# A two-layer encoder on one core: modulation weights loaded two items ahead at one even pace, and the second sequence's norm beside the first's last attention projection

## The chip, the cores and the metric

One core of a Trainium2 chip runs the whole program as one launch. The metric is device time in microseconds, the median of the runs. Five engines work side by side, each on its own list of instructions in order: TensorE (PE in the profile, its weight loads PEld), VectorE (DVE), ScalarE (ACT), GpSimd (POOL) and SyncE (SP). Weights come from DRAM: SP issues the loads of the projection weights, POOL those of the modulation weights and of parked rows.

## The reference

Two sequences of 512 tokens and width 1024 pass through the same two layers. A layer is a mixer and an MLP, each behind an RMS norm whose scale, shift and gate come from a condition vector `c`:

```python
def adaln(c, w, b):                       # w: 1024 x 6144, a layer
    mod = silu(c) @ w + b
    return split(mod, 6)                  # sh1, sc1, g1, sh2, sc2, g2

for i in range(2):
    sh1, sc1, g1, sh2, sc2, g2 = adaln(c, mod_w[i], mod_b[i])
    h = rmsnorm(x, norm1_g[i]) * (1 + sc1) + sh1
    m = retention(h, ...) if i == 0 else attention(h, ...)
    x = x + g1 * m
    h = rmsnorm(x, norm2_g[i]) * (1 + sc2) + sh2
    x = x + g2 * (square(relu(h @ w1)) @ w2)
return rmsnorm(x, final_g)
```

Retention has 4 heads (q and k of 256, v and a gate g of 512 columns a head), attention has 8 query heads and 2 key/value heads of 128.

## The kernel before

Everything is float32. An activation or weight tile of 128 x 512 is cut into a high and a low part (`split`, and `load_piece` for a weight piece of 128 x 1024: `whi` on ACT, `wlo` on DVE, line 206), and every product is three matmuls (`mm3`, lines 218 to 220).

**Retention** runs in eight steps, four heads of the first sequence and then four of the second. A step makes scores (`scores`, whose four evictions on DVE are line 517), values (4 weight pieces), the gate (4 pieces, evicted by line 533), the head's output `y` (line 549 and on), then the next head's q and k (4 pieces, with rope) in turn with four transposed products `tz` (PE line 570, DVE line 572), and the output projection `out` (4 pieces, evicted by line 586). That is 16 weight pieces a step. Step 3 also makes the second sequence's first norm (lines 261 to 291) and step 7 the first sequence's second norm (lines 310 to 313). In the text, a step runs from its first score eviction on DVE to that of the next step.

**Modulation** hides behind these steps. It is 12 chunks (6 a layer) of 8 items; an item is 128 columns, whose weights are two tiles of 128 x 512 (two loads, line 407, on POOL's queue) and which DVE multiplies and sums with the condition rows in two dots a sequence (`dot`, line 382): two dots where one sequence is left to do, otherwise four. Items wait in the list `bg`. Each weight piece calls `tick` behind its `wlo`; `tick` adds `pace` to a counter, and when that passes 1 it issues the dots of the item that is loaded (`bg_dot`) and then the loads of the next one (`bg_load`). The tiles come from the pool `f2` of eight, of which six are held (two rope tables, four condition tiles) until the last rope, in step 6. So one pair is left, and an item's loads wait on POOL for the dots of the item before. The scheduler keeps this program order where it must, and sets the place of each instruction on its engine by its own estimates.

**The wide MLP** (from about 1000 to 1600 us and from about 2060 us on) and **attention** follow. In attention the heads of the first sequence (`heads`: softmax and its product, 16 turns) are woven with a generator `fill`, one step of it a turn: the rest of the first sequence's last projection `p1` (rope and transposes), the second sequence's norm `nm1` (statistics, spread, then eight modulated tiles: lines 288, 290 and 291), its projection `q2` and then `q0`.

Of the kernel before, what the change touches and what calls it, by code (L numbers as in the profile page):

```python
# [18 lines left out]
EPS = 1e-6  # L19
ORDER_FIRST = "q0 q1 z0 q2 z1 z2 q3 z3"  # L20
ORDER = "g1 g2 g3 q0 z0 q1 z1 q2 z2 z3 q3"
PACE = 0.55
PACE_LAST = 1.0
SQ_W = 8
SQ_RAW = 3
SQ_SUM = 4
# [5 lines left out]
def kernel(  # L32
# [98 lines left out]
    def small(w):  # L131
        return sm.tile([P, w], F32, tag=f"s{w}", name=f"s{w}")
# [13 lines left out]
    bg, loaded = [], []  # L146
    pace = [0.0, 0.0]

    def bg_dot():
        if loaded:  # L150
            f, hv = loaded.pop()
            f(hv)

    def bg_load():
        if bg:
            f, g = bg.pop(0)
            loaded.append((g, f()))

    def tick(ins):
        pace[1] += pace[0]  # L160
# [4 lines left out]
            pace[1] -= 1.0  # L165

    def flush():
        while bg or loaded:
            bg_dot()
            bg_load()  # L170

    sq = {}

# [71 lines left out]
    def fetch(src, alloc=xtile, eng=nc.gpsimd):  # L245
        t = alloc()
        eng.dma_start(t, src)
        return t
# [53 lines left out]
    def stats_of(tiles):  # L302
        st = Stats()
        for x in tiles:
            st.add(x)
        return st
# [55 lines left out]
    def cond_row(s):  # L362
        halves = []
        for hf in range(2):
            c, th = sftile(), sftile()
            ld(c[0:1, :], cs[s:s + 1, hf * T:(hf + 1) * T])
            act(th[0:1, :], c[0:1, :], AF.Tanh, scale=0.5)
            stt(c[0:1, :], th[0:1, :], 1.0, c[0:1, :], ALU.add, ALU.mult)
            ps = abank()
            mm(ps, ones[0:1, :], c[0:1, :], start=True, stop=True)  # L370
            w = f2tile()
            act(w, ps, AF.Copy)
            halves.append(w)
        return halves
# [4 lines left out]
    def dot(a, w, cb, k):  # L379
        for hf in range(2):  # L380
            junk = sm.tile([P, T], BF16, tag="junk", name="junk", bufs=1)
            stt(junk, w[hf], 0.5, cb[hf], ALU.mult, ALU.mult, accum_out=a[:, 2 * k + hf:2 * k + hf + 1])  # L382

    def mod_cols(a, layer, ch, s, k0, k1):
        col = modc[layer, ch, s]
        av = a.rearrange("p (k t) -> p k t", t=2)
        c0 = layer * 48 + ch * KD
        c = col[:, k0:k1]
        tt(c, av[:, k0:k1, 0], mb_sb[:, c0 + k0:c0 + k1], ALU.add)
        tt(c, c, av[:, k0:k1, 1], ALU.add)  # L390
        gi = gain_of.get((layer, ch))
        if gi is not None:
            stt(c, c, 1.0, gn_sb[:, gi, k0:k1], ALU.add, ALU.mult)

    def new_col(layer, ch, s):
        modc[layer, ch, s] = const.tile([P, KD], F32, name=f"mc{layer}_{ch}_{s}")

    def mod_chunk(cb, layer, ch, seqs=(0, 1), alt=False):
        accs = {s: small(2 * KD) for s in seqs}
        for s in seqs:  # L400
            new_col(layer, ch, s)

        def load(k):
            get = xtile if alt and k % 2 else f2tile
            hv = [get(), get()]
            for hf in range(2):
                nc.gpsimd.dma_start(hv[hf], modw[layer, ch * KD + k][:, hf * T:(hf + 1) * T])  # L407
            return hv

        def step(k, hv):  # L410
            for s in seqs:
                dot(accs[s], hv, cb[s], k)
            if k == KD - 1:
                for s in seqs:
                    mod_cols(accs[s], layer, ch, s, 0, KD)

        for k in range(KD):
            bg.append((lambda k=k: load(k), lambda hv, k=k: step(k, hv)))

# [22 lines left out]
    def decay_strip(h, alloc=None):  # L444
        get = ld if alloc else nc.gpsimd.dma_start
        alloc = alloc or ftile
        d = dp.tile([P, 896], F32, tag="d", name="dstrip")
        for hf in range(2):
            sl = slice(hf * 448, (hf + 1) * 448)
            a, b = alloc(), alloc()  # L450
            get(a[:, 0:448], posneg[0][:, sl])
            get(b[:, 0:448], posneg[1][:, sl])
            nc.gpsimd.tensor_scalar(a[:, 0:448], a[:, 0:448], lg[:, h:h + 1], 0.0, ALU.mult, ALU.add)
            nc.gpsimd.tensor_scalar(b[:, 0:448], b[:, 0:448], lg[:, 4 + h:5 + h], 0.0, ALU.mult, ALU.add)
            strip_pool[0] = nc.gpsimd.tensor_tensor(d[:, sl], a[:, 0:448], b[:, 0:448], ALU.add)
            act(d[:, sl], d[:, sl], AF.Exp)
        return d
# [641 lines left out]
    def run(g, n=None):  # L1099
        while n is None or n > 0:  # L1100
            try:
                next(g)
            except StopIteration:
                return
            if n is not None:
                n -= 1
# [15 lines left out]
    cb = [cond_row(0), None]  # L1122
# [32 lines left out]
    for i in range(4):  # L1155
        for t in range(2):
            k = 2 * i + t
# [59 lines left out]
    for step in range(8):  # L1217
        s, n = divmod(step, 4)
        nm = None
        r.scores(n, strip)  # L1220
        if step == 3:
            with tc.issue_after(first_pool.ins):
                s1 = stats_of(fetch(xs[1][k]) for k in range(KD))
            nm = Norm(s1, lambda k: fetch(xs[1][k]),
                      modc[0, 1, 1], modc[0, 0, 1], True)
            r1 = Ret(1, None, nm.h)
        if step == 7:
            nm = Norm(stats_of(fetch(park[0][k]) for k in range(KD)), lambda k: fetch(park[0][k]),
                      modc[0, 4, 0], modc[0, 3, 0], True, keep=hparks[0][0])
            m.h[0] = nm.h  # L1230
        if step > 0:
            r.v(n)
        if nm is not None:
            nm.a()
        r.g(n, [0] if step else [3])
        if nm is not None:
            nm.c()
        r.y(n)
        if nm is not None:
            nm.m()  # L1240
        if step < 7:
            strip = decay_strip((n + 1) % 4)
        if step == 7:
            r.g(n, [1, 2, 3])
        if step < 7:
            nxt = r1 if step == 3 else r
            n1 = (n + 1) % 4
            for t in (ORDER if step else ORDER_FIRST).split():
                i = int(t[1])
                if t[0] == "q":  # L1250
                    nxt.qk(n1, i)
                elif t[0] == "z":
                    r.tz([i])
                else:
                    r.g(n, [i])
            if step == 0:
                flush()
                mod_chunk(cb, 0, 1, (1,))
                mod_chunk(cb, 0, 0, (1,))
                pace[0] = PACE  # L1260
            if step == 2:
                flush()
                mod_chunk(cb, 0, 2, (1,))
                for ch in (4, 3, 5):
                    mod_chunk(cb, 0, ch)
                for ch in (1, 0, 2, 3, 4, 5):
                    mod_chunk(cb, 1, ch)
                pace[0] = PACE_LAST
            if step == 3:
                while len(bg) > 71 or (loaded and len(bg) == 72):  # L1270
                    bg_dot()
                    bg_load()
            if step == 6:
                while len(bg) > 47 or (loaded and len(bg) == 48):
                    bg_dot()
                    bg_load()
            if step == 3:
                r.out(n, lambda o: nc.gpsimd.dma_start(park[0][o], x0[o]))
                r1.x = [fetch(xs[1][k], ptile) for k in range(KD)]
                r = r1  # L1280
            else:
                r.out(n)
        else:
            m.x[1] = r.x
            m.ups(0, 0, [0])
            r.tz([0, 1])
            m.ups(0, 0, [1])
            r.tz([2, 3])
            m.ups(0, 0, [2])
            st1 = Stats()  # L1290
            r.out(n, lambda o: st1.add(r.x[o]))
            with tc.issue_after(r.last.ins):
                m.x[0] = [fetch(park[0][k], ftile, nc.scalar) for k in range(KD)]
            m.ups(0, 0, [3])
            flush()
    f2_ctx.__exit__(None, None, None)
    wide_stage(m, st1)
# [28 lines left out]
    nm1 = Norm(st[1], lambda k: fetch(park[1][k]), modc[1, 1, 1], modc[1, 0, 1], True)  # L1326
    a1 = Att(1, nm1.h, tabs)
    p2, p0, p1 = a0.proj(2), a0.proj(0), a0.proj(1)
    q2, q0, q1 = a1.proj(2), a1.proj(0), a1.proj(1)

    def part(g, n):
        for _ in range(n):
            run(g, 1)
            yield
# [13 lines left out]
    run(zipped(p0, p1))  # L1348

    def fill():  # L1350
        yield from p1
        yield from nm1.steps(4)
        yield from part(q2, 4)
        yield from zipped(q2, q0)

    f = fill()
    weave(a0.heads(), f)
    run(f)
# [20 lines left out]
    f = fill()  # L1379
# [21 lines left out]
    f = finish(0, st[0])  # L1401
# [159 lines left out]
```

## Time and profile before

| what | us |
|---|---|
| median of 3 runs (2665.93 to 2669.35) | 2667.32 |
| the profiled execution | 2666.18 |
| its span, first to last instruction | 2664.4 |
| PE busy | 2528.7 (95%) |
| DVE busy | 1991.8 (75%) |
| ACT busy | 1120.2 (42%) |
| POOL busy | 526.2 (20%) |

Shares of the whole span hide the stages: a stage in which PE waits for DVE shows only in windows of that stage. Busy time of PE is also longer while the granted clock is low, so both are read together. In the views, `f` and `xf` are tiles (the pools' names without numbers), `pm`, `pa`, `ps` and `pt` are banks of PSUM, `junk` is the unused product of a dot, and a wait is named by the line that waits and the line or load that ended it. Each dot is two entries of line 382, the product and a short read of its sum.

### The profile page before, as it was taken

The page shows a single profiled execution, that of the slowest core. Times are in us where ns is not written, and L with a number is a line of the kernel's source. Part 1 is how long each engine was busy: PE and PEld are TensorE (multiplying, and loading weights), DVE is VectorE, ACT ScalarE, POOL GpSimd, SP SyncE. Part 2 cuts the span into 40 slices and gives each one's busy share as a digit, 9 for nine tenths or more (in the row PEclk, how much of TensorE's full clock was granted, in tenths as well). Part 3 has the DMA queues.
Part 4 walks back from the last instruction along what each step waited for, and adds up shares of the span by engine and source line. Part 5 has one row for each costly group of instructions (what it writes and reads, how often), then busy time and mean ns, then how long its engine had stood idle before and what let it go on. Part 6 is the DMA issues. An engine that isn't in the chain of part 4 may idle for free. (4 is left out here: it accounts for less than half of the span.)

```text
span 2664.4 us, 32643 instructions
## 1 busy us (share of the span) xinstructions
PE 2528.7 (95%) x11186; PEld 2056.7 (77%) x11186; DVE 1991.8 (75%) x3800; ACT 1120.2 (42%) x1949; POOL 526.2 (20%) x947
## 2 busy tenths in 40 slices
PE   6999999889897999999999999899999999999998
PEld 4888887767676777888878887678778788878887
DVE  6767577778877978666778867776876766688777
ACT  3433333222222355444444434675774444454432
POOL 2302112221212212121222200000014121242100
PEclk9999999999998999999999999899999999999999
DMA  7544454644444656444565434122337454474433
GB/s 248 190 127 138 126 168 148 205 143 146 134 150 132 210 181 213 163 154 163 171 211 164 162 114 140 53 63 76 115 122 271 157 180 144 160 277 159 139 95 103
DMA packets 133994, 414.00 MB, mean 155 GB/s; under 512 B 21250, under 2 KB 24194, under 8 KB 133828
## 3 DMA queue, kind: packets, MB, share of 16 engines
q0 software_dynamic: 68352, 224.58, 24.9%
q1 hardware_dynamic: 59284, 180.32, 21.6%
q10 hardware_dynamic: 6192, 7.02, 0.8%
q8 instruction: 88, 1.44, 0.2%
q14 instruction: 78, 0.64, 0.1%
HBM read 332.15 MB, written 79.69 MB: 155 GB/s over the span
## 5 line engine op out<-in xcount | busy, mean ns | idle before, releaser
L218 PE MATMUL pm<-r,whi 128*128 128x512 f32 x768 | 306.7, 402 | 29.8 <-DVE f L572 14.6
L205 ACT ACTIVATE whi<-raw 128x1024 fp32r<-128x1024 f32 x174 | 183.6, 1057 | 339.1 <-DMA raw<-in_wri_dram 106.4
L220 PE MATMUL pm<-r,wlo 128*128 128x512 f32 x768 | 304.6, 397 | 9.1 <-DVE wlo L206 9.1
L219 PE MATMUL pm<-r,whi 128*128 128x512 f32 x768 | 305.6, 398 | 5.5 <-DVE r L313 5.4
L382 DVE SCALAR_TENSOR_TENSOR junk<-f,f 128x512 bf16<-128x512 f32 x344 | 239.6, 696 | 94.1 <-DMA f<-in_modw_dram 91.0
L206 DVE TENSOR_TENSOR wlo<-raw,whi 128x1024 fp32r<-128x1024 f32 x174 | 216.9, 1247 | 89.6 <-ACT whi L205 89.0
L225 ACT ACTIVATE wh<-rawq 128x512 fp32r<-128x512 f32 x228 | 142.5, 629 | 286.6 <-PE pm L667 159.7
L225 ACT ACTIVATE wh<-sum 128x512 fp32r<-128x512 f32 x208 | 129.9, 629 | 280.0 <-PE pa L667 178.2
L666 PE MATMUL pa<-r,wh 128*128 128x512 f32 x624 | 242.7, 389 | 0.0
L667 PE MATMUL pa<-r,wh 128*128 128x512 f32 x624 | 242.7, 389 | 0.0
L668 PE MATMUL pa<-r,wh 128*128 128x512 f32 x624 | 242.7, 389 | 0.0
L407 POOL DMA_DIRECT2D f<-in_modw_dram x200 | 108.2, 541 | 596.6 <-DVE junk L382 495.8
L218 PEld LDWEIGHTS pm<-r,whi 128*128 128x128 f32 x768 | 147.3, 192 | 65.0 <-issue 15.9
L666 PE MATMUL pm<-r,wh 128*128 128x512 f32 x468 | 182.6, 390 | 1.9 <-ACT wh L225 1.9
L668 PE MATMUL pm<-r,wh 128*128 128x512 f32 x468 | 182.1, 389 | 0.0
L667 PE MATMUL pm<-r,wh 128*128 128x512 f32 x468 | 182.1, 389 | 0.0
L220 PEld LDWEIGHTS pm<-r,wlo 128*128 128x128 f32 x768 | 147.7, 192 | 42.2 <-DVE wlo L206 11.2
L218 PE MATMUL pa<-whi,r 128*128 128x512 f32 x440 | 174.2, 399 | 5.1 <-ACT whi L205 4.2
L219 PEld LDWEIGHTS pm<-r,whi 128*128 128x128 f32 x768 | 147.9, 193 | 39.8 <-DVE r L313 8.7
L219 PE MATMUL pa<-wlo,r 128*128 128x512 f32 x440 | 174.0, 396 | 0.6 <-DVE wlo L206 0.6
L226 DVE TENSOR_TENSOR wh<-sum,wh 128x512 fp32r<-128x512 f32 x208 | 141.4, 685 | 44.1 <-ACT wh L225 42.7
L220 PE MATMUL pa<-whi,r 128*128 128x512 f32 x440 | 173.6, 394 | 0.0
(277 smaller groups left out, 5978.8 us busy)
## 6 DMA issues: line engine op xcount, KB each, us to landing
rawq<-in_w_dram SPq DMA_DIRECT2D x144, 512.0 KB, 3.9
f<-in_modw_dram POOLq DMA_DIRECT2D x200, 256.0 KB, 3.4
raw<-in_wri_dram SPq DMA_DIRECT2D x92, 512.0 KB, 3.8
r<-hhpark POOLq DMA_DIRECT2D x142, 256.0 KB, 4.1
hhpark<-f POOLq DMA_DIRECT2D x96, 256.0 KB, 2.9
hhpark<-p POOLq DMA_DIRECT2D x88, 256.0 KB, 2.3
raw<-in_wro_dram SPq DMA_DIRECT2D x32, 512.0 KB, 3.7
xf<-park POOLq DMA_DIRECT2D x48, 256.0 KB, 3.4
```

Of the source, the lines that this page charges most:

```text
L205: act(hi, raw, AF.Copy)
L206: ins = tt(lo, raw, hi.bitcast(F32), ALU.subtract)
L218: mm(ps, a[0], b[0], start=first, stop=False)
L219: mm(ps, a[0], b[1], start=False, stop=False)
L220: return mm(ps, a[1], b[0], start=False, stop=last)
L225: split.last = act(hi, src_f32, AF.Copy)
L226: split.dve = tt(lo, src_f32, hi.bitcast(F32), ALU.subtract)
L382: stt(junk, w[hf], 0.5, cb[hf], ALU.mult, ALU.mult, accum_out=a[:, 2 * k + hf:2 * k + hf + 1])
L407: nc.gpsimd.dma_start(hv[hf], modw[layer, ch * KD + k][:, hf * T:(hf + 1) * T])
L666: mm(ps, a[0], b[0], start=first and k == 0, stop=False, **more)
L667: mm(ps, a[0], b[1], start=False, stop=False, **more)
L668: mm(ps, a[1], b[0], start=False, stop=k == n - 1, **more)
```

## The change

In the modulation, `PACE` 0.55 (steps 0 to 2) and `PACE_LAST` 1.0 (from the end of step 2) become one pace of 0.88 over all 96 items that are left after step 0. `bg_load` may keep two items loaded where their tiles come from different pools: items carry a `home`, and the first four chunks of layer 1 take every second item's tiles from the pool `x` of three buffers, which the norms of steps 3 and 7 use too. The chunks of layer 0, and the last two of layer 1, still have the one pair of `f2`. The flushes become `bg_until(n)`, which empties the list to n items. In attention, `fill` takes one step of `p1` and one of `nm1` a turn, four turns in all, where it took seven.

```diff
-PACE = 0.55
-PACE_LAST = 1.0
+PACE = 0.88
...
     def bg_dot():
         if loaded:
-            f, hv = loaded.pop()
+            f, hv, _ = loaded.pop(0)
             f(hv)
 
     def bg_load():
-        if bg:
-            f, g = bg.pop(0)
-            loaded.append((g, f()))
+        while bg and (not loaded or (len(loaded) == 1 and loaded[0][2] != bg[0][2])):
+            f, g, home = bg.pop(0)
+            loaded.append((g, f(), home))
+
+    def bg_until(n):
+        while len(bg) + len(loaded) > n:
+            bg_dot()
+            bg_load()
...
     def flush():
-        while bg or loaded:
-            bg_dot()
-            bg_load()
+        bg_until(0)
...
-            bg.append((lambda k=k: load(k), lambda hv, k=k: step(k, hv)))
+            bg.append((lambda k=k: load(k), lambda hv, k=k: step(k, hv), alt and k % 2))
...
                 mod_chunk(cb, 0, 0, (1,))
-                pace[0] = PACE
-            if step == 2:
-                flush()
                 mod_chunk(cb, 0, 2, (1,))
                 for ch in (4, 3, 5):
                     mod_chunk(cb, 0, ch)
                 for ch in (1, 0, 2, 3, 4, 5):
-                    mod_chunk(cb, 1, ch)
-                pace[0] = PACE_LAST
+                    mod_chunk(cb, 1, ch, alt=ch < 4)
+                pace[0] = PACE
+            if step == 2:
+                bg_until(80)
             if step == 3:
-                while len(bg) > 71 or (loaded and len(bg) == 72):
-                    bg_dot()
-                    bg_load()
+                bg_until(72)
             if step == 6:
-                while len(bg) > 47 or (loaded and len(bg) == 48):
-                    bg_dot()
-                    bg_load()
+                bg_until(48)
...
     def fill():
-        yield from p1
-        yield from nm1.steps(4)
+        h1 = nm1.steps(4)
+        for i in range(4):
+            run(p1, 1)
+            run(h1, 1)
+            yield
+        run(p1)
+        run(h1)
         yield from part(q2, 4)
         yield from zipped(q2, q0)
```

Each engine's number of instructions is the same in both. DVE's order holds these dots in steps 1 to 6 and behind the first score of step 7: before 18, 22, 44, 64, 64, 66 and 54; now 28, 39, 52, 62, 56, 56 and 33. Lines 206 to 1068 of the kernel before stand two lines lower in the changed one.

The first place is POOL's list of loads in step 5. Before, each pair of `f2` follows the other, all in the same two buffers:

```order
L407 DMA f2_5428<-in_modw_dram 128x512
L407 DMA f2_5429<-in_modw_dram 128x512
L407 DMA f2_5470<-in_modw_dram 128x512
L407 DMA f2_5471<-in_modw_dram 128x512
L407 DMA f2_5512<-in_modw_dram 128x512
L407 DMA f2_5513<-in_modw_dram 128x512
```

Now a pair of `f2` and a pair of `x` take turns, and because `x` has a third buffer, one tile of each `x` pair is loaded a turn earlier still:

```order
L409 DMA f2_5606<-in_modw_dram 128x512
L409 DMA f2_5607<-in_modw_dram 128x512
L409 DMA xf_5649<-in_modw_dram 128x512
L409 DMA xf_5861<-in_modw_dram 128x512
L409 DMA f2_5706<-in_modw_dram 128x512
L409 DMA f2_5707<-in_modw_dram 128x512
L409 DMA xf_5862<-in_modw_dram 128x512
L409 DMA xf_5987<-in_modw_dram 128x512
```

What moved: the load of an item now stands behind the dots of the item two before it, not of the one before.

The second place is DVE in step 5, from the end of the head's statistics to the first gate evictions (L554 to L557 is the chain that scales the head's output). Before:

```order
L241 SCALAR_TENSOR_TENSOR s4_5719<-s4_5718 128x4
L382 SCALAR_TENSOR_TENSOR junk_5807,s16_3097<-f2_5769,f2_162 128x512
L242 SCALAR_TENSOR_TENSOR s4_5717<-s4_5719,s4_5717 128x4
L382 SCALAR_TENSOR_TENSOR junk_5809,s16_3097<-f2_5770,f2_171 128x512
L557 SCALAR_TENSOR_TENSOR s4_5728<-s8_5650,s4_5717 128x4
L382 SCALAR_TENSOR_TENSOR junk_5811,s16_3098<-f2_5769,f2_923 128x512
L382 SCALAR_TENSOR_TENSOR junk_5813,s16_3098<-f2_5770,f2_928 128x512
L382 SCALAR_TENSOR_TENSOR junk_5853,s16_3097<-f2_5815,f2_162 128x512
L206 TENSOR_TENSOR wlo_5950<-raw_5947,whi_5949 128x1024
L533 SCALAR_TENSOR_TENSOR f_5798<-f_5798,pm_5773 128x512
```

Now:

```order
L243 SCALAR_TENSOR_TENSOR s4_5807<-s4_5806 128x4
L244 SCALAR_TENSOR_TENSOR s4_5805<-s4_5807,s4_5805 128x4
L559 SCALAR_TENSOR_TENSOR s4_5816<-s8_5738,s4_5805 128x4
L208 TENSOR_TENSOR wlo_6030<-raw_6027,whi_6029 128x1024
L535 SCALAR_TENSOR_TENSOR f_5890<-f_5890,pm_5865 128x512
L384 SCALAR_TENSOR_TENSOR junk_6033,s16_1422<-f2_5941,f2_162 128x512
```

What moved: no dot stands in this chain any more; the weight piece and the gate's eviction stand ahead of the next four dots.

The third place is PE among the first heads of attention, where the second sequence's first projection (`pa`, L218 before, L220 now) begins. `pt` and `ps` are the heads' own work. Before it is PE's row 7024:

```order
L1064 MATMUL pt_15129<-ident_92,p_14950 128x128
L218 MATMUL ps_15071<-r_14256,r_14800 128x512
L219 MATMUL ps_15071<-r_14257,r_14800 128x512
L220 MATMUL ps_15071<-r_14256,r_14801 128x512
L218 MATMUL pa_15182<-whi_15188,r_15017 128x512
L1064 MATMUL pt_15138<-ident_92,p_14911 128x128
```

Now it is row 6936:

```order
L220 MATMUL ps_14793<-r_14247,r_14475 128x512
L221 MATMUL ps_14793<-r_14248,r_14475 128x512
L222 MATMUL ps_14793<-r_14247,r_14476 128x512
L1066 MATMUL pt_14869<-ident_92,p_14647 128x128
L1066 MATMUL pt_14869<-ident_92,p_14660 128x128
L220 MATMUL pa_15024<-whi_15030,r_14841 128x512
L1066 MATMUL pt_14878<-ident_92,p_14621 128x128
```

What moved: the projection begins 88 PE instructions earlier. On DVE the low part of the first modulated tile, for which the three-matmul product waits, comes 76 instructions behind the heads' first maximum, where it came 121 behind it. From the end of this stage on, and in the wide MLP, the lists are the same.

## Rows read from the trace of the kernel before

**Rows 1.** Page: span, PE, granted clock in 40 slices.

```profile
span 2664.4 us, 32643 instructions
PE 2528.7 (95%) x11186; PEld 2056.7 (77%) x11186; DVE 1991.8 (75%) x3800; ACT 1120.2 (42%) x1949; POOL 526.2 (20%) x947
...
PEclk9999999999998999999999999899999999999999
```

**Rows 2.** Busy time by engine in steps 1 to 7 (header names the columns).

```profile
core 0: us, PE busy (x) PEld busy (x) DVE busy (x) ACT busy (x) POOL busy (x), PEclk, DMA share, GB/s
...
168.00:273.10 105.10, 105.10 (x473) 87.16 (x472) 67.78 (x122) 32.16 (x42) 16.70 (x28) 1.00 0.44 134
273.10:383.10 110.00, 108.23 (x485) 89.32 (x485) 68.99 (x129) 32.29 (x42) 18.86 (x32) 1.00 0.44 136
383.10:506.80 123.70, 110.91 (x481) 88.65 (x480) 99.40 (x210) 42.53 (x59) 37.45 (x63) 0.97 0.55 179
506.80:628.60 121.80, 112.06 (x472) 89.95 (x471) 98.11 (x223) 31.69 (x42) 26.77 (x46) 0.95 0.50 158
628.60:751.60 123.00, 109.79 (x472) 88.73 (x472) 97.48 (x221) 31.65 (x43) 25.26 (x43) 0.96 0.46 145
751.60:877.50 125.90, 109.82 (x462) 88.14 (x463) 96.16 (x221) 31.28 (x42) 26.24 (x45) 0.95 0.45 144
877.50:975.00 97.50, 89.21 (x384) 70.69 (x383) 89.44 (x219) 44.55 (x66) 24.20 (x45) 0.96 0.62 198
```

**Rows 3.** Waits of DVE in steps 4 to 6: total, times, longest.

```profile
DVE junk L382 <- DMA f<-in_modw_dram: 70.4, 46, 4.5
```

**Rows 4.** Waits of PE in steps 4 to 6.

```profile
PE pm L218 <- DVE f L572: 14.6, 3, 5.0
PE pm L218 <- DVE f L533: 7.1, 2, 4.8
PE pm L220 <- DVE wlo L206: 5.4, 3, 2.3
```

**Rows 5.** Timeline of DVE and of POOL, 638 to 652 us.

```profile
641.57 0.69 DVE L382 SCALAR_TENSOR_TENSOR junk<-f,f 128x512 bf16<-128x512 f32 x1
...
645.91 0.69 DVE L382 SCALAR_TENSOR_TENSOR junk<-f,f 128x512 bf16<-128x512 f32 x1 [3.64 <-DMA f<-in_modw_dram]
...
641.83 0.54 POOL L407 DMA_DIRECT2D f<-in_modw_dram  x1 [5.50 <-DVE junk L382]
642.56 0.54 POOL L407 DMA_DIRECT2D f<-in_modw_dram  x1 [0.20 <-issue]
```

**Rows 6.** Windows, steps 4 to 6: the six stretches at low clock.

```profile
584.40:591.20 6.80, 4.62 (x11) 3.69 (x12) 6.66 (x15) 1.58 (x2) 1.14 (x3) 0.50 0.50 155
...
sum 37.60, PE 25.77 PEld 20.23 DVE 29.80 ACT 10.72 POOL 10.49; mean PE 4.30 PEld 3.37 DVE 4.97 ACT 1.79 POOL 1.75
```

**Rows 7.** Windows of line 382 alone, step 4; two entries a dot.

```profile
506.80:628.60 121.80, 46.01 (x130) 0.95 0.50 158
```

**Rows 8.** Waits of DVE for these loads, step 3, then steps 1 and 2.

```profile
DVE junk L382 <- DMA f<-in_modw_dram: 10.8, 7, 4.7
...
DVE junk L382 <- DMA f<-in_modw_dram: 7.0, 4, 2.4
```

**Rows 9.** Waits of PE in step 7.

```profile
PE pm L219 <- DVE r L313: 5.4, 7, 1.1
PE pm L279 <- DVE f L273: 2.2, 1, 2.2
```

**Rows 10.** Windows of the first sequence's heads; one row of PE's timeline.

```profile
1696.60:1727.00 30.40, 23.14 (x89) 15.53 (x89) 26.09 (x80) 23.43 (x70) 0.54 (x1) 0.78 0.04 9
1727.00:1748.30 21.30, 16.47 (x81) 11.68 (x81) 18.75 (x43) 16.22 (x33) 3.23 (x6) 1.00 0.32 99
1748.30:1800.00 51.70, 51.65 (x256) 41.98 (x255) 38.47 (x95) 41.45 (x92) 0.54 (x1) 1.00 0.15 46
...
1747.98 0.50 PE L218 MATMUL pa<-whi,r 128*128 128x512 f32 x1 [0.98 <-ACT r L290]
```

## The prediction

> **What bounds the kernel now.** I read the page first. PE is busy for 2528.7 of 2664.4 us, and its clock is a 9 in almost every slice [rows 1], so all that a change of order can win is PE's 136 us of idle time and what the low clock costs. Then the windows by step show where that lies. In step 1 PE is busy for the whole 105.10 us, at a granted clock of 1.00. Steps 4 to 6 do the same work and take 121.8, 123.0 and 125.9 us, and here the vector engine (DVE) is busy for 98.11, 97.48 and 96.16 us [rows 2]. The waits of DVE in these three steps name one thing: 70.4 us, in 46 waits, for the modulation weights [rows 3]. Its busy time, 291.8 us, and these waits make 362.2 of 370.7 us. So DVE has no slack there, and PE waits for what DVE delivers late: the transposed products (line 572), the gate (line 533), the low weight parts (line 206) [rows 4].
>
> The timeline shows how a wait comes about. A dot, the last of its item, starts at 641.57 us; POOL, which had waited for the dots, issues the next two loads at 641.83 and 642.56; the next item's first dot starts at 645.91, after 3.64 us in which DVE did nothing [rows 5]. With one pair of tiles that stall lies between any two items that come close together. A wait of PE costs a second time: in the last 2 us of the gap of 5.0 us before line 218 [rows 4] the granted clock falls to 0.50, which is 1.2 GHz, and stays there for 6.8 us; PE works for 4.62 us of them [rows 6], at half its rate, so 2.3 us more are lost.
>
> **The change part by part.** The sum starts from the profiled execution, 2666.2 us (span 2664.4, 1.8 around it); the median of the runs shown is 1.1 above.
>
> *Steps 4 to 6, what could be won.* PE is busy for 112.06, 109.79 and 109.82 us, so it idles for 9.7, 13.2 and 16.1: 39.0. In the six stretches at the low clock PE works for 25.77 us [rows 6]; half of that, 12.9, is the clock's. Without both the three take 318.8 us, 106.3 each, which fits the 105.1 and 108.2 us of PE work in steps 1 and 2. So 51.9 us are the most that these steps can give.
>
> *Steps 4 to 6, DVE's new list.* A dot costs 46.01 us over 65 of them, 0.71 [rows 7]. There are now 62, 56 and 56 where there were 64, 64 and 66, so 1.4, 5.7 and 7.1 us go, and the list is 96.7, 91.8 and 89.1 us long. The stall was 70.4 us over 48.5 items of four dots, 1.45 an item. In the order, the first five items of step 4 and the last seven of step 6 still have one pair. If each pays 1.45 again (bounds: nothing, and the 4.5 of the longest wait), the list with its stalls is 104.0, 91.8 and 99.3 us. For items with two pairs I take no stall (bounds: none, and 1.45 again): a load comes 4.3 us behind the dot that frees its tiles [rows 5], and between that dot and the one that needs it stands a whole item, four dots of 0.71, besides the weight piece, and an even pace leaves 14 items to a step. All three lists are now shorter than PE's 106.3, so PE becomes the bound.
>
> *What stays idle.* Not everything goes, since DVE's work comes in bunches. The nearest rows are step 2, where DVE is busy for 68.99 us and PE idles for 1.8, and step 7, where DVE is busy for 89.44 of 97.5 us and PE idles for 8.3 [rows 2]; 7.6 us of step 7's waits come from its norm [rows 9], which steps 4 to 6 don't have. By the length of their lists I leave 7, 4 and 6 us, the clock's share in them: 17 (bounds: 0, as in step 1, and 30, three times some 10 for a step like step 7 with its clock). So steps 4 to 6 give 51.9 - 17 = **35 us**.
>
> Weighed against a page: by the Trainium skill, "Perfetto Trace Analysis", section "Identifying the Most-Contended Engine", busy time of matmuls is no fair measure of how near TensorE is to its limit, and that of weight loads is. By weight loads, step 1 is full at 87.16 of 105.10 us, 0.829, and steps 4 to 6 hold 266.8 us of them [rows 2], so their floor is 321.7 and not 318.8, and the most to be won 49.0; the sum would end at 2633. Here the two agree within 3 us, because the clock's share has been taken out of the busy time first; read plainly, 331.7 us busy of 370.7, it would have left only 39.0 to win.
>
> *Steps 1 to 3, which get the dots that steps 4 to 7 lose.* Step 1 gains 10 dots, 7.1 us, against 37.3 us in which DVE is idle: nothing. Step 2 gains 17 dots, 12.1 us, and seven of its items now have four dots on one pair, at most 7 x 1.45 = 10.2 us of stalls; DVE goes from 68.99 to about 91 of 110 us [rows 2]. That is like step 5, where I leave 4 us, and 1.8 are there already: cost 2 (bounds: 0 and 10, a loss like step 7's). Step 3 gains 8 dots, 5.7 us, and its 13 items on one pair pay about 18.9 us of stalls where 10.8 are seen [rows 8]: 13.8 us more on an engine that is busy for 99.40 us and waits 10.8 for loads out of 123.7, so 13.5 us of other waiting can cover it. Those waits stand elsewhere in the step than the dots, so I take a third: cost **4** (bounds: 0 and 13.8).
>
> *Step 7.* 33 dots instead of 54: 14.9 us less on DVE. PE idles there for 8.3 us, and the clock of 0.96 adds 2 to 4 [rows 2], but 5.4 of it stands at the norm's low parts and 2.2 at its spread [rows 9], and two items are still dotted between those lines. I take **4** (bounds: 0 and 11). The flushes cost nothing: at 0.88 the items that each calls for are done before it.
>
> *Attention.* The heads of the first sequence start at 1696.6. Up to 1727 PE idles for 7.3 of 30.4 us at a clock of 0.78, up to 1748.3 for 4.8 of 21.3, and then hardly at all [rows 10], because the second sequence's projection starts at 1747.98 and fills every gap. That start waits for the norm's first low part, 121 DVE instructions behind the heads' first maximum, and now 76. At the same pace, 51.4 x 76/121 = 32 us, it comes at about 1729. Of the 4.8 us, the part behind 1729 goes: **4**. The first 30 us stay as they are, since DVE is busy there for 26.09 of 30.4 us and its list only becomes denser. Bounds: 5 us won, and 7 lost, if the projection's matmuls stand in PE's list ahead of the heads' work and wait for DVE as long as PE waits now up to 1727.
>
> *The sum.* 2666.2 - 35 + 2 + 4 - 4 - 4 = 2629; with the 1.1 us between profile and median, **2630**.
>
> **The rivals.**
> - *Nothing stays idle.* Steps 4 to 6 run at 106.3 us each, as steps 1 and 2 do. For it: the order of PE's work is that of steps 1 and 2, where DVE keeps up. Against it: there DVE's list is 65% of the step, here 85 to 99%. 17 us more than forecast, and the 4 of step 3: about 2609.
> - *DVE stays the pace.* The wait for loads goes, but the transposed products and the gate still come late, because rope, evictions and dots fall into the same part of a step. For it: PE's largest waits are for these [rows 4]. Against it: DVE reached them late after some 20 us of stalls a step. With 40 us left instead of 17, 2653.
> - *Slower: the stall moves.* All items between 16 and 47 have one pair and most now have four dots. If each waits as long as the longest did, 4.5 us, step 3's list is 105.1 + 13 x 4.5 = 163.6 us against 123.7 (40 lost), step 2's 81.1 + 31.5 = 112.6 (3 lost), step 4's 96.7 + 22.5 = 119.2 (3 won) and step 6's 120.6 (5 won); step 5 wins 14 and the rest 8: 2680. It decides from a mean wait of about 4.1 us. Against it: the mean is 1.45, and the pace is lower than the one under which that was seen.
> - *No change.* PE's waits in steps 4 to 6 have another cause, and only attention and step 7 give a little: 2662 to 2667. Against it: 362 of 371 us of DVE are accounted for.
>
> **How the numbers follow.** Forecast 0.64, nothing idle 0.15, DVE the pace 0.12, no change 0.04, slower 0.05. The likeliest's own range is 2614 to 2646. The range 2604 to 2655 takes in most of the first three. A measurement of this kernel tells about 0.2% (5 us) from no change; that gives faster 0.90, same 0.05, slower 0.05.
>
> **What would show it.** Right: in steps 5 and 6 DVE's waits for modulation weights fall below 10 us a step from 23, PE is idle for less than 8 us each, and each takes 107 to 114 us; step 3 stays between 122 and 132; step 7 loses a few us; the second sequence's projection starts some 20 us earlier after the heads begin. Wrong: steps 4 to 6 keep 120 us with DVE busy for all of it, or waits for those weights of 20 us and more appear in steps 2 and 3, and PE's gaps with them.

## The result and the profile after

| | us |
|---|---|
| before, median of 4 runs (2662.38 to 2669.35) | 2666.62 |
| changed, median of 4 runs (2615.62 to 2628.67) | 2625.09 |
| ratio, with its 95% interval | 0.984 (0.9811 to 0.9869) |
| the changed kernel's profiled execution, and its span | 2615.62, 2613.8 |

The profiled execution is the fastest of the four, 9.5 us under their median. A second profile of the same kernel, taken with the experiments, has a span of 2620.7; where one execution could mislead, both are given.

The page after (its head, PE's line and the granted clock) answers to [rows 1]:

```profile
span 2613.8 us, 32647 instructions
PE 2518.2 (96%) x11186; PEld 2052.8 (79%) x11186; DVE 1992.3 (76%) x3800; ACT 1119.3 (43%) x1949; POOL 522.2 (20%) x947
PEclk9999999999999999999999999999999999999999
```

DVE does the same work, 1992 us; PE's idle time fell from 135.7 to 95.6 us, and its busy time by 10.5. About half of these 10.5 us is the clock's, if half of the time at the low clock is lost, as the prediction takes it: at 0.50 PE was busy for 70.9 us of the whole span before and is for 60.6 now, and half of the difference is 5.2. What makes up the rest isn't shown. The windows of steps 0 to 7 after (columns as in [rows 2]; the last one ends at the same PE instruction as the last row there):

```profile
99.00:170.40 71.40, 69.51 (x313) 56.79 (x312) 57.98 (x123) 20.95 (x28) 21.75 (x36) 1.00 0.57 179
170.40:277.80 107.40, 105.94 (x476) 87.51 (x475) 74.77 (x144) 32.27 (x42) 22.02 (x38) 1.00 0.50 155
277.80:386.00 108.20, 107.92 (x482) 88.67 (x481) 81.24 (x163) 31.99 (x42) 19.82 (x34) 1.00 0.47 147
386.00:518.10 132.10, 115.67 (x473) 89.43 (x473) 102.91 (x230) 41.06 (x58) 37.88 (x66) 0.92 0.54 174
518.10:630.30 112.20, 106.81 (x473) 86.86 (x473) 95.72 (x219) 33.01 (x43) 26.39 (x43) 1.00 0.54 167
630.30:733.10 102.80, 102.80 (x463) 85.19 (x462) 93.34 (x203) 31.93 (x42) 21.99 (x38) 1.00 0.54 162
733.10:841.20 108.10, 107.54 (x482) 88.72 (x481) 90.64 (x199) 32.03 (x42) 23.04 (x40) 1.00 0.52 160
841.20:931.10 89.90, 85.20 (x375) 69.36 (x375) 76.30 (x176) 43.45 (x65) 18.78 (x35) 0.98 0.58 179
```

Steps 4 to 6 take 323.1 us where they took 370.7. In step 5 PE is busy for all of its 102.8 us while DVE is still busy for 93.34 of them: the bound has changed hands. Step 3 went the other way, from 123.7 to 132.1. The waits of DVE and of PE in steps 4 to 6 after show the same, beside [rows 3] and [rows 4]:

```profile
DVE junk L384 <- DMA f<-in_modw_dram: 16.6, 12, 3.7
```

```profile
PE pa L221 <- DVE r L228: 2.3, 1, 2.3
PE pa L220 <- DVE r L228: 1.5, 1, 1.5
PE pm L572 <- DVE f L473: 1.1, 2, 0.5
```

70.4 us of waits for modulation weights have become 16.6 (10.7 in step 4, 6.0 in step 6, none in step 5; 18.6 in the second profile), and the long waits of PE for transposed products and the gate are gone. POOL's and DVE's timelines after, in step 5, show how:

```profile
639.10 0.54 POOL L409 DMA_DIRECT2D f<-in_modw_dram  x1 [6.63 <-DVE junk L384]
639.84 0.54 POOL L409 DMA_DIRECT2D f<-in_modw_dram  x1 [0.20 <-issue]
```

```profile
639.58 0.69 DVE L384 SCALAR_TENSOR_TENSOR junk<-xf,f 128x512 bf16<-128x512 f32 x1
643.53 0.69 DVE L384 SCALAR_TENSOR_TENSOR junk<-f,f 128x512 bf16<-128x512 f32 x1
```

DVE goes on at 639.58 with the other pair (`xf`), and its four dots and a weight piece fill the time until 643.53, when the first dot on the new pair of `f` runs without a wait. It is tight: 3.7 us after the second load was issued.

In step 3, PE's largest wait before and after, and the two stretches at the low clock after (windows, columns as before):

```profile
PE pm L279 <- DVE f L273: 4.7, 1, 4.7
```

```profile
PE pm L281 <- DVE f L275: 6.0, 1, 6.0
```

```profile
418.10:428.30 10.20, 5.91 (x12) 4.01 (x13) 7.06 (x21) 0.60 (x1) 1.07 (x2) 0.50 0.60 179
489.80:500.00 10.20, 7.84 (x17) 5.24 (x18) 7.92 (x16) 0.84 (x2) 3.22 (x6) 0.50 0.60 200
```

Line 281 (279 before) is the spread of the second sequence's norm. 16 dots of step 3 stand ahead of it in both kernels, and 27 now stand ahead of the norm's first low part, where 20 stood. Of the 8.4 us that step 3 lost, 3.6 are idle time of PE (12.8 before, 16.4 now) and 4.8 are busy time: the granted clock fell from 0.97 to 0.92, and the kernel before had one stretch of 6.8 us at the low clock in this step and the first 0.9 us of another.

The heads of attention, from the first maximum at 1655.1 on, and PE's row at which the projection begins, beside [rows 10]:

```profile
1655.10:1685.50 30.40, 23.83 (x96) 15.74 (x96) 27.64 (x84) 25.34 (x73) 1.08 (x2) 0.83 0.06 18
1685.50:1706.80 21.30, 21.30 (x108) 17.36 (x107) 20.34 (x44) 17.86 (x35) 3.22 (x6) 1.00 0.26 75
```

```profile
1682.79 0.50 PE L220 MATMUL pa<-whi,r 128*128 128x512 f32 x1 [1.29 <-ACT r L292]
```

The projection starts 27.7 us behind the heads' beginning, 51.4 before; the 4.8 us of idle time in the second stretch are gone, the first stretch is as it was.

### The profile page after: what moved, and what is told of

Its sections match the earlier page's. It is cut to its first block, busy times and chain, and to the rows that moved or that the text cites. A ratio compares the mean times of both kernels' runs of the same rounds, so it can differ in the third digit from the quotient of the medians.

```text
span 2613.8 us, 32647 instructions
## 1 busy us (share of the span) xinstructions
PE 2518.2 (96%) x11186; PEld 2052.8 (79%) x11186; DVE 1992.3 (76%) x3800; ACT 1119.3 (43%) x1949; POOL 522.2 (20%) x947
## 5 line engine op out<-in xcount | busy, mean ns | idle before, releaser
L220 PE MATMUL pm<-r,whi 128*128 128x512 f32 x768 | 304.2, 399 | 13.3 <-ACT r L1180 5.8
L208 DVE TENSOR_TENSOR wlo<-raw,whi 128x1024 fp32r<-128x1024 f32 x174 | 214.6, 1234 | 94.3 <-ACT whi L207 93.7
L384 DVE SCALAR_TENSOR_TENSOR junk<-f,f 128x512 bf16<-128x512 f32 x280 | 194.3, 694 | 52.1 <-DMA f<-in_modw_dram 49.2
L409 POOL DMA_DIRECT2D f<-in_modw_dram x168 | 90.7, 540 | 474.5 <-DVE junk L384 378.2
L220 PEld LDWEIGHTS pm<-r,whi 128*128 128x128 f32 x768 | 145.9, 190 | 48.3 <-ACT r L1180 6.2
L220 PE MATMUL pa<-whi,r 128*128 128x512 f32 x440 | 174.4, 399 | 5.5 <-ACT whi L207 4.2
```

The source lines that it names most:

```text
L208: ins = tt(lo, raw, hi.bitcast(F32), ALU.subtract)
L220: mm(ps, a[0], b[0], start=first, stop=False)
```

## The experiments

**Theory A**, the prediction's: the load stall made DVE late, the second pair takes it away, and then PE is the pace in steps 4 to 6. **Rival B**: the lower, even pace does it alone. The further letters stand in the expectations. The times of the kernels are medians, the columns of steps come from one profile each; 2663.2, 2663.3 and 2665.0 are those of the kernel before beside the three groups of runs (the first four kernels below, the next three, the last four). The table is what the text below reads: widths of steps from the first score evictions, the dots between those of step 3, and "step 7", from there to the first product of the wide MLP's own stage (line 666 before).

| kernel | us | ratio (95%) | dots, step 3 | step 3 | steps 4-6 | step 7 |
|---|---|---|---|---|---|---|
| before | | | 44 | 123.7 | 370.7 | 193.4 |
| changed, again | 2624.3 | 0.9853 (0.9836-0.9870) | 52 | 132.4 | 327.4 | 186.9 |
| one pair | 2650.3 | 0.9949 (0.9935-0.9964) | 52 | 133.3 | 353.5 | 187.4 |
| old paces | 2633.5 | 0.9880 (0.9861-0.9899) | 67 | 140.2 | 339.9 | 181.0 |
| old fill | 2628.3 | 0.9870 (0.9852-0.9888) | 52 | 132.5 | 327.3 | 189.5 |
| rest in step 3 | 2600.1 | 0.9764 (0.9739-0.9789) | 39 | 119.6 | 322.2 | 186.8 |
| tiny dots | 2575.4 | 0.9668 (0.9643-0.9692) | 51 | 116.6 | 313.6 | 183.9 |
| no load wait | 2679.6 | 1.0066 (1.0047-1.0085) | 49 | 119.2 | 313.4 | 186.8 |
| even step 3 | 2605.5 | 0.9780 (0.9764-0.9796) | 44 | 126.3 | 320.8 | 185.6 |
| rest only | 2614.3 | 0.9812 (0.9795-0.9829) | 40 | 122.6 | 325.5 | 191.4 |
| rest in 3 and 7 | 2597.1 | 0.9752 (0.9736-0.9768) | 39 | 118.5 | 321.8 | 186.6 |
| all two pairs | 2606.8 | 0.9788 (0.9772-0.9805) | 39 | 122.2 | 316.6 | 191.8 |

### The changed kernel again

> The changed kernel once more, as the base for the runs beside it. Both theories: 2615 to 2630 us, 36 to 51 us under the kernel before; steps 4 to 6 again about 323 us together (370.7 before). If its runs spread by 10 us again, the profile should show which stage they spread in.

2624.3, with steps 4 to 6 at 327.4. Of the 7 us between its profile and the first one, 5.6 are there before step 7, most of them in step 6, where PE is idle for 3.9 us here and for 0.6 there:

```profile
734.60:846.80 112.20, 108.33 (x477) 89.12 (x476) 93.29 (x199) 31.82 (x42) 23.12 (x40) 0.98 0.50 154
```

### One pair

```diff
-                    mod_chunk(cb, 1, ch, alt=ch < 4)
+                    mod_chunk(cb, 1, ch)
```

> The even pace of 0.88 is kept, all modulation items have the one pair of tiles again. Theory A (the loads' stall was what made the vector engine late, and the second pair takes it away): 62, 56 and 56 dots plus 1.45 us of stall for each of 14 to 15 items a step make a list of about 117, 112 and 110 us, so steps 4 to 6 take about 342 us in place of 323, the waits for modulation weights there come back to some 60 us, and the kernel takes 2640 to 2648 us. Rival B (the even pace alone did it, by taking dots out of steps 4 to 6): within 5 us of the changed kernel, 2620 to 2630.

The waits come back as A said, 58.1 us in steps 4 to 6 (waits of DVE), and with them PE's waits for the transposed products, 15.1 us after 14.6 in the kernel before [rows 4]:

```profile
DVE junk L384 <- DMA f<-in_modw_dram: 58.1, 45, 3.8
```

```profile
PE pm L220 <- DVE f L574: 15.1, 3, 5.4
```

The windows of these steps are those of a late DVE, with a lower clock:

```profile
519.00:640.20 121.20, 110.67 (x473) 90.05 (x472) 94.15 (x215) 32.91 (x43) 25.25 (x43) 0.94 0.50 155
640.20:757.20 117.00, 109.26 (x477) 88.72 (x476) 92.41 (x203) 31.94 (x42) 24.02 (x38) 0.97 0.46 143
757.20:872.50 115.30, 107.87 (x470) 88.01 (x469) 92.69 (x203) 31.93 (x42) 25.12 (x40) 0.97 0.48 152
```

B falls. The even pace has a share all the same: with one pair steps 4 to 6 take 353.5 us, 17.2 less than before, and step 3 pays 9.6 for it. A's 342 us were 11 too few, though the waits have the size that it gave: in step 5 DVE's busy time, 92.4, and its 19.5 us of waits for loads make 111.9 of the 117.0, and its other waits come on top.

### Old paces

```diff
-PACE = 0.88
+PACE = 0.55
+PACE_LAST = 1.0
...
-                bg_until(80)
+                bg_until(72)
+                pace[0] = PACE_LAST
```

> The second pair of tiles is kept, the two old paces are back (0.55 in steps 1 and 2, 1.0 from the end of step 2). Theory A: steps 1 to 3 as in the kernel before (105, 110, 124), step 4 half with stalls, steps 5 and 6 without, together some 336 us, so with attention's part 2622 to 2632, nearly all of the gain. Rival B: dots still 64, 64 and 66 in steps 4 to 6, so they keep more than 355 us together, and the kernel takes 2648 to 2660.

Steps 4 to 6 follow A, and B falls here too: they hold 203 dots, more than the 194 of the kernel before, and take 30.8 us less than there. Step 3 doesn't follow: it holds 67 dots, not the 44 of the kernel before, and takes 140.2 us (its window):

```profile
382.30:522.50 140.20, 115.46 (x474) 88.80 (x472) 111.44 (x260) 41.32 (x58) 40.85 (x72) 0.93 0.53 172
```

The reason lies in the diff: the kernel before empties its list at the end of step 2 with 80 items still to come, and this one empties it to 72. So steps 2 and 3 get 31 and 67 dots where 22 and 44 stood, and behind the first score of step 7 only 13 are left of 54. The run brings the old paces back but not the old spread, and so it doesn't price the even spread beside two pairs.

### Old fill

```diff
-        h1 = nm1.steps(4)
-        for i in range(4):
-            run(p1, 1)
-            run(h1, 1)
-            yield
-        run(p1)
-        run(h1)
+        yield from p1
+        yield from nm1.steps(4)
```

> The changed kernel with the old order in attention (the first projection's rest first, then the second norm). Theory A: attention's part of the change is worth 4 (forecast) to 8 us (the profiles of before and after differ there by 8), so 2629 to 2633 with a changed kernel at 2625. Rival: the gaps that the earlier projection fills come back later in the stage and the old order costs nothing, within 2 us of the changed kernel.

4.0 us, as forecast, though the intervals of the two ratios overlap. The trace carries it: from the heads' first maximum to the next wide product 402.0 us here and 397.6 in the changed kernel's profile of the same group. The second stretch of the heads has its 4.8 us of idle time back:

```profile
1691.40:1712.70 21.30, 16.48 (x82) 11.75 (x81) 18.78 (x44) 16.24 (x33) 3.22 (x6) 1.00 0.33 99
```

### Rest in step 3

```diff
-PACE = 0.88
+PACE = 1.0
...
     for step in range(8):
         s, n = divmod(step, 4)
+        if step == 3:
+            pace[0] = 0.0
...
         r.g(n, [0] if step else [3])
+        if step == 3:
+            pace[0] = 1.0
...
                 bg_until(72)
+                pace[0] = 0.88
```

> The changed kernel with another spread of the same items: pace 1.0 in steps 1 and 2, none through the first five weight pieces of step 3 (where the second sequence's norm is made), 1.0 for the rest of step 3, then 0.88. On the vector engine's list step 2 gets 48 dots instead of 39, step 3 gets 39 instead of 52, 12 of them ahead of the norm's spread instead of 16. Theory A (in step 3 the vector engine is the pace, so a dot there costs its 0.71 us, and in step 2 it is not): step 3 falls from 132 to about 123, step 2 rises by 0 to 3, and the kernel takes 2614 to 2620 against 2624. Rival C (step 3's loss is the one wait for the norm's spread and the stalls of the one pair, whatever the number of dots): step 3 stays at 128 or more, and the kernel takes 2621 to 2627.

Better than A said: 24 us under the changed kernel. Step 3 lost 12.8 us; the 13 dots fewer are 6.7 us of it (line 384 is busy there for 29.39 us, 36.07 in the changed kernel's profile) and DVE's waits for loads 4.6 (6.8 after 11.4). C falls. Its window, and PE's wait for the spread:

```profile
382.10:501.70 119.60, 111.50 (x486) 90.33 (x485) 98.60 (x199) 42.64 (x59) 33.35 (x59) 0.98 0.57 184
```

```profile
PE pm L281 <- DVE f L275: 2.7, 1, 2.7
```

The other gains, 4.9 us ahead of step 3 and 5.2 in steps 4 to 6, are about what two executions of one list differ by (below). Whether the fuller steps 1 and 2 have a share in the whole is asked in "rest only".

### Tiny dots

```diff
-            stt(junk, w[hf], 0.5, cb[hf], ...
+            stt(junk[:, 0:1], w[hf][:, 0:1], 0.5, cb[hf][:, 0:1], ...
```

> Work left out: every dot multiplies one column of 512; all loads and their waits stay. Theory A (in steps 5 and 6 of the changed kernel the tensor engine is the pace, in steps 3 and 4 the vector engine): steps 5 and 6 together stay at 208 to 214 us, step 3 falls to 112 to 120 and step 4 to about 107, so some 20 us in all, 2600 to 2608. Rival D (the vector engine is still the pace everywhere, just a shorter list): each of steps 4 to 6 falls by a further 5 us or more, below 102, and the kernel goes under 2595.

It went to 2575, under both numbers, but not by D's way: DVE is busy for 64 us in steps 5 and 6 instead of some 93, and yet they take 105.2 us each, 210.4 together (210.9 and 214.6 in the changed kernel's profiles), with PE busy throughout (windows of the two steps). That is PE's pace. About half of what A had missed lies ahead of step 3, which starts 13 to 14 us earlier than in the changed kernel (372.6 against 386.0 and 387.0); 6.9 of them are there before the first score eviction of step 0 (92.1 against 99.0), so the dots at the very start have a price too.

```profile
592.40:697.60 105.20, 105.20 (x473) 87.20 (x472) 64.34 (x203) 32.26 (x42) 21.94 (x38) 1.00 0.51 159
697.60:802.80 105.20, 105.20 (x473) 87.21 (x472) 64.38 (x205) 32.26 (x42) 23.02 (x40) 1.00 0.52 164
```

### No load wait

```diff
-            stt(junk, w[hf], 0.5, cb[hf], ...
+            stt(junk, cb[hf], 0.5, cb[hf], ...
```

> Data changed: every dot reads a condition tile in place of the loaded weights, so no dot waits for a load; the loads are still issued, and the number and length of the dots stay. Theory A (in steps 3 and 4, whose items still have one pair, the 12 us of waits for loads in each are on the path): step 3 falls from 132 to 120 to 125 and step 4 from 113 to about 108, the kernel takes 2606 to 2614. Rival E (these waits only take the place of others, since the tensor engine is waited for there too): less than 5 us, 2619 to 2626.

Neither: 55 us slower than the changed kernel. Steps 3 and 4 did fall, to 119.2 and 104.0, as A said. But steps 0 to 2 rose to 80.1, 132.9 and 153.9 us. POOL's timeline shows loads with nothing to hold them but the landing of the one before, and behind them in its list the tables of the next head's decay strip (line 453; the scores are multiplied by the strip). ACT waits for the strip, and behind ACT's wait stand the gate's tanh and with it DVE's eviction and PE (rows of POOL, ACT and PE):

```profile
256.39 0.54 POOL L409 DMA_DIRECT2D f<-in_modw_dram  x1 [1.06 <-DMA f<-in_modw_dram]
257.95 0.54 POOL L409 DMA_DIRECT2D f<-in_modw_dram  x1 [1.03 <-DMA f<-in_modw_dram]
258.48 0.54 POOL L453 DMA_DIRECT2D f<-in_posneg_dram  x1
```

```profile
265.39 0.58 ACT L458 ACTIVATE dstrip<-dstrip 128x448 f32<-128x448 f32 x1 [36.75 <-POOL dstrip L457]
```

```profile
269.56 0.80 PE L220 MATMUL pm<-r,whi 128*128 128x512 f32 x1 [25.92 <-DVE f L535]
```

The lists aren't those of the changed kernel: since no dot needs a load here, 93 loads stand ahead of the second strip's tables in POOL's list, where the changed kernel has 38, and 169 ahead of the third's, where it has 66. So the loss is that of another order, and the run doesn't price the stalls for the kernel. In steps 4 to 6, behind that, it takes 313.4 us, as "tiny dots" does.

### Even step 3

As "rest in step 3", with these lines in place of the rest:

```diff
+        if step == 3:
+            pace[0] = 0.69
```

> As the run with the rest in step 3 (2600 us), but with no rest: pace 1.0 in steps 1 and 2, an even 0.69 through step 3, then 0.88. Step 3 holds 44 dots, 17 of them ahead of the norm's spread (39 and 12 with the rest, 52 and 16 in the changed kernel). Theory A (the number of dots in step 3 decides, 0.71 us each): step 3 at about 124, 12 dots' worth less 4 from the 132 of the changed kernel and 4 more than with the rest, and the kernel at 2602 to 2608. Theory F (their place decides: dots ahead of the spread keep the tensor engine waiting and cost its clock): step 3 keeps the wait of 5 to 6 us for the spread and 128 or more, and the kernel takes 2610 to 2618.

A's number for the kernel, 2605.5; step 3 at 126.3 lies between A's 124 and F's 128. The wait for the spread stays at 5.7 us, so F has that wait right, and the place of the dots has a share: 5 dots more than with the rest cost 6.7 us.

### Rest only

As "rest in step 3", with pace 0.88 in steps 1 and 2.

> The changed kernel with the rest in step 3 alone: pace 0.88 in steps 1 and 2, none through the first five pieces of step 3, 1.0 for the rest of it, then 0.88. Step 3 holds 40 dots, 12 ahead of the spread, as in the run at 2600 us; step 2 keeps 34, and step 7 gets 49 instead of 29. Theory A: step 3 at 119 to 123 again, and step 7 pays for its 20 dots more with 3 to 8 us, so 2605 to 2612. Rival G (the 24 us came from steps 1 and 2 being filled, not from step 3): step 3 above 126, and the kernel above 2615.

Step 3 at 122.6 with 40 dots: that is A's, and G falls for step 3. The kernel's 2614.3 lies above A's 2605 to 2612, and G is right in part: the rest alone wins 10.0 of the 24 us. The other 14 come with the fuller steps 1 and 2, since without them step 7 pays 4.6 us for 20 dots more, and step 4, which has more items on one pair, 9.7 (117.2 against 107.5; its waits for loads are 19.1 us against 7.2).

### Rest in 3 and 7

```diff
-        if step == 3:
+        if step in (3, 7):
```

at both places of the rest.

> The run at 2600 us with a second rest, through the first five pieces of step 7, where the first sequence's second norm is made, and 1.0 after it. 13 dots instead of 21 stand ahead of that norm's spread. Theory A: step 7 has some 3 us of waits for its norm left, so 0 to 4 us less, 2596 to 2600. Rival: the dots come back beside the projection at the end of step 7 and cost there, 2601 to 2606.

2597.1, the lowest of the kernels that leave no work out, but its interval overlaps with that of the single rest, and step 7 took 186.6 against 186.8 us. That a second rest helps isn't shown.

### All two pairs

```diff
-                    mod_chunk(cb, 1, ch, alt=ch < 4)
+                    mod_chunk(cb, 1, ch, alt=True)
```

in the kernel with the rest in step 3.

> The run at 2600 us with the second pair for all of layer 1's items, the last two chunks (in steps 6 and 7) too. Theory A: step 6 has 5 us of waits for loads left and step 7 shares the pool with its norm, so nothing that can be measured, 2596 to 2604. Rival: the last items take the pool's buffers from the norm's fetches of parked rows in step 7, its spread comes late, and the kernel takes 2604 to 2612.

Step 6 falls by 4.4 us (109.8 to 105.4), and step 7 gives 5.0 back (186.8 to 191.8), with PE's wait for the norm's spread at 4.6 us instead of 3.8: nothing won. The kernel's 2606.8 lies in the rival's range and not in A's, and step 7 went the rival's way, but the wait that the rival names grew by 0.8 us only. The some 6 us between the two kernels stand in steps 0 to 3, where their lists are the same.

## Why the prediction was right, step by step

The forecast was 2630, the measured 2625, and the mechanism is shown for steps 4 to 6: without the second pair the waits for loads, DVE's lateness and PE's waits all come back. By the medians of one group (2663.2 before, 2624.3 changed, 38.9 won) the second pair is worth 26.0 us. The other 12.9 (2663.2 less the 2650.3 of "one pair") are those of the pace and of attention; attention's part is 4.0 by "old fill", so about 9 are left for the even pace beside one pair. Beside two pairs its worth isn't shown, since "old paces" moved dots into step 3 as well. That the sum came so near has some luck in it: steps 4 to 6 and step 7 gave more than forecast, and steps 0, 1 and 3 cost more. The terms, against both profiles of the changed kernel:

| term | forecast | measured |
|---|---|---|
| steps 4 to 6 | -35 | -47.6, -43.3 |
| steps 0 and 1, and the start | 0 | +4.7, +4.7 |
| step 2 | +2 | -1.8, -0.8 |
| step 3 | +4 | +8.4, +8.7 |
| step 7 | -4 | -7.4, -6.5 |
| attention | -4 | -9.7, -7.5 |

The wide MLP and the end add +3.0 and +1.2. (The stage of attention took 402.0 us with the old fill and 405.1 before, so only some 4 of its number are the change's.)

- **"17 left idle" was too much.** In steps 4 to 6 PE is idle for 5.4, 0 and 0.6 us in the first profile and for 5.0, 0 and 3.9 in the second; so the rival "nothing stays idle" came true in step 5, and in step 6 in one of the two. Step 5 took 102.8 and 102.4 us, less than the 107 to 114 that were named as a sign. The nearest rows, steps 2 and 7, were the wrong neighbours: in step 7 it is the norm that makes PE wait, and where there is none a DVE list of 90% of the step kept up.
- **The floor** of 318.8 us was a little high too. "Tiny dots" gives 313.6 for steps 4 to 6, 104.5 each, so halving the busy time at the low clock didn't take out all that goes when PE needn't wait; what the rest is isn't shown. The weight loads of its last two steps, 87.20 and 87.21 us, are 0.829 of 105.2, the very share of step 1 before. By the rule weighed ahead, from the Trainium skill, "Perfetto Trace Analysis", section "Identifying the Most-Contended Engine", the busy share of weight loads tells how near TensorE is to its limit, and the trace agrees in so far as the share of a full step came out the same. The 321.7 worked out by that share was further off than 318.8, since weight loads take longer at the low clock as well: 12 of them 3.69 us [rows 6], 0.31 each, where 472 took 87.16 in step 1 [rows 2], 0.185 each.
- **Step 3's term was mis-sized**, at half of what it cost. The sum had two thirds of DVE's longer list covered by other waits, and it put nothing in for the clock. By the halving that it used for steps 4 to 6, the clock makes more than half of the 8.4 us: PE is busy for 13.8 us at the low clock in this step (5.91 + 7.84, above), and half of that, 6.9, is lost, where it was 2.4 at most before. So the step ended at 132.1 and 132.4 us, just beyond the 122 to 132 that were named as a sign. By dots, step 3 takes 118.5 to 122.2 us with 39 of them, 122.6 with 40, 126.3 with 44 (123.7 in the kernel before), 132.1 to 133.3 with 52 and 140.2 with 67: from 39 (mean 120.1) to 67 that is 20.1 / 28 = 0.72 us a dot, as much as a dot takes on DVE [rows 7], with norm and dots on one engine. It is a mean and not a fixed price: from 52 to 67 it is some 0.5, from 39 to 44 in "even step 3" more than 1. The price holds more than the dots' own time: between "rest in step 3" and "old paces" DVE is busy for 12.8 us more and idle for 7.8 more, and the clock falls from 0.98 to 0.93. How much of it the clock makes between these two wasn't separated. The load waits that I had feared there hardly grew, 11.6 us after 10.8 [rows 8].
- **Step 2** bore its dots for nothing, and even 48 of them in the runs with pace 1.0. The start and steps 0 and 1 take 4.7 us more, which the sum had at nothing. Most of it is where step 2 begins on DVE: PE has done 1080 instructions there and not 1067, and 13 of them are 2.9 us at the rate of step 1's row [rows 2]. The waits for loads in steps 1 and 2 grew from 7.0 [rows 8] to 14.3 us.
- **Stalls of one pair**, forecast as 1.45 us an item, are 11.6 us over the 13 items of step 3, 0.9 each, so the rival "slower" never came near its 4.1.
- **Step 7**: 186.0 to 189.5 us with 33 dots, 193.4 with 54, 191.4 with 49, 181.0 with 13, so about 0.3 us a dot from the ends; forecast 4 / 21 = 0.2. The kernels with 33 dots differ by 3.5 us among themselves, half of what was won.
- **Attention**: the projection starts 23.7 us earlier after the heads begin (forecast some 20), and 4.0 to 4.4 us are won (forecast 4). By its row [rows 10] the start waits for ACT's high part (line 290) and not, as said ahead, for DVE's low part, which starts 0.3 us later (1748.31). Both are made from the same product on DVE, line 288, so the count of DVE's list still gave about the right time.

The pattern that started it, the same gap again and again on an engine that should be full, is one that the Trainium skill names in "Perfetto Trace Analysis", section "Optimization Strategy", as a possible sign of too few buffers. "One pair" and the changed kernel agree with that: 58.1 against 16.6 us of waits for one buffer pair more.

## What to carry to other kernels

Background work on an engine is free only in stages in which that engine has room, so spread it by the room of each stage and not evenly: here an even pace put dots beside a norm at some 0.7 us each, while step 2, ahead of it, took 48 at no price that could be seen. Look at which engine's busy time and waits fill a stage before you choose between a second buffer and less work; here the buffer was worth 26 us, and the even spread about 9 with one buffer. A run that takes a wait away can also change the order of the lists: compare them before you put the time down to the wait.

## What was not expected of the hardware

- Loads that nothing holds back were no gift: in "no load wait" POOL issued them some 1.6 us apart, 55 more of them than in the changed kernel stood ahead of a strip's tables, and these came so late that ACT sat for 36.75 us.
- The kernels "rest in step 3", "rest in 3 and 7" and "all two pairs" have the same order on every engine up to step 5, and yet reach the first score eviction of step 5 at 609.2, 605.7 and 615.9 us. Only a small part of it is the clock: between 100 and 600 us PE is busy at the low clock for 6.8, 5.0 and 10.2 us, and half of that is lost, so it makes at most 2.6 of the 10.2 us between the last two. The rest stays open. So a difference of 5 us in these steps between two executions shows nothing by itself. The changed kernel's runs spread over 13 us, which fits that.
